# Moving operands of the FFN in six groups of rows, each starting at another remainder of 128 bytes

## The chip, the cores and the metric

The kernel runs on one core of a Trainium2 chip. Times are microseconds (us) of device time for one execution; three timed runs of the kernel before are given with their median, and one further execution was profiled.

## The reference

One decoder block over a sequence of 256 tokens and 2048 channels, all in float32: a conditioning vector gives shift, scale and gate; two token mixers (Mamba-2 SSD and Gated DeltaNet) run in parallel and are merged; then comes the feed-forward part (FFN), with which this case deals:

```python
def swiglu(h, w_gate_up, w_down):
    gate, up = jnp.split(h @ w_gate_up, 2, axis=-1)
    return (jax.nn.silu(gate) * up) @ w_down

h = modulate(rms_norm(x, norm_ffn_w[layer]), shift_f, scale_f)
x = x + gate_f[:, None, :] * swiglu(h, w_gate_up[layer], w_down[layer])
return rms_norm(x, final_norm_w)
```

`h` is 256 x 2048, the hidden width is 5632.

## The kernel before

Activations lie transposed: channels on the 128 partitions, in rows of 256 tokens. A row is 256 float32 values, 1024 bytes on each partition. `h` has 16 rows (KT), the hidden layer 44 (FT).

Each float32 product is made of three matmuls in the type float32r. A weight block `raw` (128 x 1024, eight tiles of 128 x 128) comes in by DMA; ScalarE casts it to `hi` (line 146), VectorE makes the rest `lo = raw - hi` (line 148). The activations are split in the same way, into `h2h` and `h2l` for the first half of the FFN and `fh` and `fl` for the second. For each weight tile and row there are three matmuls, with weights `hi`, `hi`, `lo` as the stationary operand and a row of `h2h`, `h2l`, `h2h` (or `fh`, `fl`, `fh`) as the moving one: lines 216 to 218 in `lin_items`, lines 239 to 241 in `quad_items`. A block is so 24 matmuls. The gate/up half has 176 blocks (`w_gu`; the first twelve by `quad_items`), 4224 matmuls; the down half has 88 (`w_dn`), 2112 matmuls; together 6336.

`ffn_post` (lines 1146 to 1155) works on each of the 44 gate/up pairs when its sum is done: tanh on ScalarE, two products on VectorE, then `A.copy(fh[:, j, :], th)` and `V.tensor_sub(fl[:, j, :], ...)` write row j. Blocks are loaded ahead by `pump` (up to four of them ready), and each engine runs its instructions in the order in which the program gives them.

The tiles of the FFN are made at lines 1176 to 1181, when the pools of the mixers have been closed. A tile `off` of 48 words stands first and shifts all that follow it. By the program's layout the pool `ff` begins at byte 82432 of a partition, a multiple of 512, so that `h2h` starts at 82624, `h2l` at 99008, `fh` at 115392 and `fl` at 160448. Since a row is 1024 bytes, every row of these four tiles starts at remainder 64 of 128. The same remainder holds for the moving operands of the earlier stages: `hh` and `hl` (input projections, lines 216 to 218 as well), `yh` and `yl` (mixer outputs), `mh` and `ml` (merged, for `w_o`). The weight blocks `hi` and `lo` all start at a multiple of 512. In `z_items` (lines 262 to 264) the roles are turned round: there a block of weights is moving, 512 columns of it, at remainder 0.

Lines 1184 to 1191 fill `h2h` and `h2l` row by row: VectorE makes `htmp`, ScalarE writes the row of `h2h`, VectorE that of `h2l`.

Of the kernel before, what the change touches and what calls it, by code (L numbers as in the profile page):

```python
# [10 lines left out]
F32 = mybir.dt.float32  # L11
F32R = mybir.dt.float32r
# [7 lines left out]
P = 128  # L20
D = 2048
S = 256
KT = D // P
# [3 lines left out]
FT = 44  # L27
# [23 lines left out]
NCA = 2  # L51
LZ = 2

OFF = 48

VB_ADA = 0
VN_MIX = 96
# [11 lines left out]
C_NSL = 2  # L69
C_LV = 6  # L70
C_I16 = C_LV * P + 3 * 64


@with_exitstack
def block_kernel(ctx: ExitStack, tc: tile.TileContext, xT, cvec, vec, dskip, consts,
# [44 lines left out]
    def vcol(i):  # L120
        return vs[:, i:i + 1]
# [33 lines left out]
    def pump():  # L155
        while items and len(ready) < LA + 1:
            load_next()
        did = False
        if ready and ready[0][2] <= st_["done"]:
            mm, post, need, sync, hi, lo = ready.popleft()  # L160
            if sync:
                finish_posts()
            mm(hi, lo)
            posts.extend(post)
            st_["mm"] += 1
            did = True
        st_["wait"] -= 1.0
        if st_["gen"] is None and gens and gens[0][1] <= st_["mm"]:
            finish_posts()
            st_["gen"] = gens.popleft()  # L170
            st_["wait"] = 0.0
        if st_["gen"] is not None and (st_["wait"] <= 0.0 or not did):
            try:
                st_["wait"] = max(st_["wait"], -0.99) + next(st_["gen"][0]) * st_["gen"][2]
            except StopIteration:
                st_["gen"] = None
                st_["done"] += 1
        if posts:
            posts.popleft()()
        while len(posts) > PQ:  # L180
            posts.popleft()()
        st_["pumped"] += 1
        if side and st_["side"] and st_["pumped"] % st_["side"] == 0:
            side.popleft()()

    def flush():
        while items or ready or gens or st_["gen"] is not None:
            pump()
        finish_posts()
# [14 lines left out]
    def lin_items(blocks, xh, xl, nk, done, need=0, sync=False, late_need=0):  # L204
        hold = {}
        def mk(bi):
            def mm(hi, lo):
                ah, al = (xh(), xl()) if callable(xh) else (xh, xl)
                if bi == 0:
                    hold["ps"] = plin.tile([P, 2, S], F32, tag="lin", name="ps_lin")  # L210
                ps = hold["ps"]
                for j in range(BLK):
                    t, kt = divmod(bi * BLK + j, nk)
                    s = slice(j * P, (j + 1) * P)
                    h_ = ah[kt // 8][:, kt % 8, :] if isinstance(ah, list) else ah[:, kt, :]
                    T_.matmul(ps[:, t, :], hi[:, s], h_, start=kt == 0, stop=False)  # L216
                    T_.matmul(ps[:, t, :], hi[:, s], al[:, kt, :], start=False, stop=False)  # L217
                    T_.matmul(ps[:, t, :], lo[:, s], h_, start=False, stop=kt == nk - 1)  # L218
            return mm
        for bi, src in enumerate(blocks):  # L220
            last = bi == len(blocks) - 1
            post = [lambda f=f: f(hold["ps"]) for f in done] if last else []
            add_item(src, mk(bi), post, late_need if last and late_need else need, sync and bi == 0)
# [81 lines left out]
    def sq_finish():  # L305
        ps = bank("ps_sq", (P, S))
        for i, k in enumerate("ab"):
            for t in range(2):
                T_.matmul(ps, ones, sqa[k][:, t, :], start=i + t == 0, stop=i + t == 2)
        return ps  # L310

    def rstd_T(pool, ps):
        r = pool.tile([P, S], F32, tag="rstd", name="rstd")
        A.activation(r, ps, AF.Sqrt, scale=1.0 / D, bias=EPS)
        V.reciprocal(r, r)
        return r
# [12 lines left out]
    def ada_fin(j0, j1):  # L329
        V.tensor_tensor(ada[:, j0:j1], ada2[:, j0:j1, 0], ada2[:, j0:j1, 1], ADD)  # L330
        V.tensor_tensor(ada[:, j0:j1], ada[:, j0:j1], vs[:, VB_ADA + j0:VB_ADA + j1], ADD)
# [7 lines left out]
    with tc.tile_pool(name="st", bufs=1) as st:  # L339
# [97 lines left out]
        r = rstd_T(st, ps)  # L437
# [10 lines left out]
        for q in range(1, 4):  # L448
# [9 lines left out]
            if q == 2:  # L458
# [6 lines left out]
                lv = st.tile([P, 3, 64], F32, name="lv")  # L465
                nc.sync.dma_start(lv, consts[:, C_LV * P:C_I16].rearrange("p (a b) -> p a b", b=64))
                V.tensor_copy(lvm, lv)
# [163 lines left out]
    def gdn_mix(hu, unit):  # L631
        if hu == 0:
            pools["gp"] = gs.enter_context(tc.tile_pool(name="gp", bufs=1))
            pools["gsm"] = gs.enter_context(tc.tile_pool(name="gsm", bufs=2))
            pools["i16"] = pools["gp"].tile([64, 256], F32, name="i16")
            nc.sync.dma_start(pools["i16"], consts[0:64, C_I16:C_I16 + 256])
        gp, gsm = pools["gp"], pools["gsm"]
# [485 lines left out]
    def res_post(j, gate, pool):  # L1123
        def f(ps):
            x2 = pools["accs"]
            for t in range(2):
                i = 2 * j + t
                V.scalar_tensor_tensor(x2[:, i, :], ps[:, t, :], gate[:, i:i + 1], x2[:, i, :], MUL, ADD)
            sq = pool.tile([P, 2, S], F32, tag="th" if j else "cacc", name="sq", bufs=1 if j or pool is not gl_ else NCA)
            A.activation(sq, x2[:, 2 * j:2 * j + 2, :], AF.Square)  # L1130
            if j == 0:
                sqa["a"] = sq
            elif j < 7:
                G.tensor_tensor(sqa["a"], sqa["a"], sq, ADD)
            else:
                sqa["b"] = sq
        return [f]
# [36 lines left out]
    phase_a.close()  # L1174

    with tc.tile_pool(name="ff", bufs=1) as ff:
        ff.tile([P, OFF], F32, name="off")
        h2h = ff.tile([P, KT, S], F32R, name="h2h")
        h2l = ff.tile([P, KT, S], F32R, name="h2l")
        fh = ff.tile([P, FT, S], F32R, name="fh")  # L1180
        fl = ff.tile([P, FT, S], F32R, name="fl")
        F_.update(h=h2h, l=h2l, fh=fh, fl=fl, ff=ff)
        tmps = {}
        for t in range(KT + 1):
            if t < KT:
                tmps[t] = ff.tile([P, S], F32, tag="fth", name="htmp", bufs=2)
                V.scalar_tensor_tensor(tmps[t], x2[:, t, :], wsf[:, t:t + 1], rf, MUL, MUL)
                A.activation(h2h[:, t, :], tmps[t], AF.Identity, bias=ada[:, 48 + t:49 + t])
            if t > 0:
                V.scalar_tensor_tensor(h2l[:, t - 1, :], tmps[t - 1], ada[:, 47 + t:48 + t],  # L1190
                                       h2h[:, t - 1, :].bitcast(F32), ADD, SUB)
        while items:
            pump()
        while side:
            side.popleft()()
        gf = ff.tile([P, KT], F32, name="gf")
        for j in range(8):
            lin_items([w_dn[j, b] for b in range(11)], fh, fl, FT, res_post(j, gf, ff))
        ada_fin(80, 96)
        V.tensor_scalar(gf, ada[:, 80:96], 0.5, None, MUL)  # L1200
        while len(items) > 20:
            pump()
        for t in (1, 4, 7):
            A.activation(x2[:, t, :], x2[:, t, :], AF.Identity, scale=vcol(VN_FIN + t))
        A.activation(dum, ones[:, 0:1], AF.Sqrt)
        flush()
        r = rstd_T(ff, sq_finish())
        for t in range(KT):
            if t in (1, 4, 7):
                G.tensor_tensor(x2[:, t, :], x2[:, t, :], r, MUL)  # L1210
            else:
                V.scalar_tensor_tensor(x2[:, t, :], x2[:, t, :], vcol(VN_FIN + t), r, MUL, MUL)
            if t % 2 == 1:
                (nc.sync if t % 4 == 1 else nc.scalar).dma_start(out[:, t - 1:t + 1, :], x2[:, t - 1:t + 1, :])
# [101 lines left out]
```

## Time and profile before

| | us |
|---|---|
| timed runs | 2779.04, 2808.68, 2811.40 |
| their median | 2808.68 |
| the profiled execution | 2783.04 |
| its span (first to last instruction) | 2781.3 |
| TensorE busy in the span | 2673.4 (96%) |
| FFN matmuls, first start to last start | 2037.8 to 2765.9 |

In the profile PE is TensorE's matmul, PEld its weight load, DVE is VectorE, ACT ScalarE, POOL GpSimd. Matmuls are pipelined: the duration of one (276 ns in the FFN) is longer than the distance from its start to the next start. So the pace of the engine is read from starts, and is called the pitch here: the time from one matmul's start to that of the next. The ends of matmuls are modelled.

### The profile page before, as it was taken

What the parts mean: (1) busy time and instruction counts of PE and PEld (TensorE: products, weight loads), DVE (VectorE), ACT (ScalarE), POOL (GpSimd) and SP (SyncE); (2) the same over time, 40 slices, a digit from 0 to 9 for tenths busy, and PEclk for the clock granted to TensorE, in tenths of its full rate; (3) what the DMA queues carried; (4) which work ended last, traced back from release to release, by engine and by line L of the source; (5) the groups of instructions that cost most, each with busy time, mean ns of one, the idle gap of its engine ahead of it and who ended that gap; (6) DMA issues with size and microseconds to landing.
All of it is one profiled execution on the core that took longest, in us unless ns stands there. A gap on an engine that the chain in (4) does not pass through costs nothing.

```text
span 2781.3 us, 51762 instructions
## 1 busy us (share of the span) xinstructions
PE 2673.4 (96%) x20930; PEld 2549.9 (92%) x20930; DVE 1885.3 (68%) x2794; ACT 1372.3 (49%) x2250; POOL 289.3 (10%) x684
## 2 busy tenths in 40 slices
PE   6999999999999999999999999999989999999998
PEld 5998898989899898889898999999989999999997
DVE  6887757667685766767766777777666666655444
ACT  3335454645454454546565565664444444444442
POOL 0000312213021221300000000002100000000000
PEclk8999999999999999999999999999999999999999
DMA  8986646465564646545555555556756666665553
GB/s 324 331 311 213 214 161 223 143 209 170 182 207 152 223 145 207 165 168 172 204 197 186 193 182 183 189 188 240 247 173 229 226 224 232 220 205 196 192 188 137
DMA packets 183283, 566.89 MB, mean 204 GB/s; under 512 B 34754, under 2 KB 43778, under 8 KB 183042
## 3 DMA queue, kind: packets, MB, share of 16 engines
q1 hardware_dynamic: 154306, 552.56, 58.2%
q10 hardware_dynamic: 28736, 11.01, 1.5%
q8 instruction: 164, 2.69, 0.4%
q14 instruction: 77, 0.62, 0.1%
HBM read 552.49 MB, written 11.01 MB: 203 GB/s over the span
## 4 chain that ended last, share of the span: by engine, by line
PE 61%; issue 12%; DVE 11%; POOL 8%; ACT 5%; DMA 3%; SPq 0%; ACTq 0%; DVEq 0%; POOLq 0%
PE ps_lin L216 13%; PE ps_lin L217 13%; PE ps_lin L218 13%; DVE lo L148 4%; PE ps_z L262 3%; PE ps_z L264 2%; PE ps_z L263 2%; POOL tm L726 2%; POOL Gt L728 2%; DVE cacc L290 2%; DMA raw<-in_w_g 1%; ACT hi L146 1%; DVE araw L326 1%; DMA araw<-in_w_ada 1%; PE td L777 1%
## 5 line engine op out<-in xcount | busy, mean ns | idle before, releaser
L148 DVE TENSOR_TENSOR lo<-raw,hi 128x1024 fp32r<-128x1024 f32 x825 | 1010.3, 1235 | 551.1 <-ACT hi L146 544.3
L146 ACT CAST hi<-raw 128x1024 fp32r<-128x1024 f32 x825 | 857.9, 1049 | 479.1 <-PE ps_lin L217 298.9
L216 PE MATMUL ps_lin<-hh,hi 128*128 128x256 f32 x1792 | 507.6, 283 | 1.0 <-DVE accg L574 1.0
L218 PE MATMUL ps_lin<-hh,lo 128*128 128x256 f32 x1792 | 499.6, 279 | 7.4 <-DVE lo L148 7.4
L217 PE MATMUL ps_lin<-hl,hi 128*128 128x256 f32 x1792 | 499.0, 278 | 0.0
L216 PE MATMUL ps_lin<-h2h,hi 128*128 128x256 f32 x1312 | 362.1, 276 | 0.0
L217 PE MATMUL ps_lin<-h2l,hi 128*128 128x256 f32 x1312 | 362.1, 276 | 0.0
L218 PE MATMUL ps_lin<-h2h,lo 128*128 128x256 f32 x1312 | 362.1, 276 | 0.0
L218 PEld LDWEIGHTS ps_lin<-hh,lo 128*128 128x128 f32 x1792 | 338.5, 189 | 8.8 <-DVE lo L148 8.8
L216 PEld LDWEIGHTS ps_lin<-hh,hi 128*128 128x128 f32 x1792 | 338.2, 189 | 5.0 <-issue 3.6
L217 PEld LDWEIGHTS ps_lin<-hl,hi 128*128 128x128 f32 x1792 | 338.8, 189 | 4.0 <-issue 2.6
L216 PE MATMUL ps_lin<-yh,hi 128*128 128x256 f32 x896 | 260.7, 291 | 18.8 <-DVE accg L574 17.0
L217 PE MATMUL ps_lin<-yl,hi 128*128 128x256 f32 x896 | 253.0, 282 | 0.0
L218 PE MATMUL ps_lin<-yh,lo 128*128 128x256 f32 x896 | 252.9, 282 | 0.0
L216 PEld LDWEIGHTS ps_lin<-h2h,hi 128*128 128x128 f32 x1312 | 246.3, 188 | 0.0
L217 PEld LDWEIGHTS ps_lin<-h2l,hi 128*128 128x128 f32 x1312 | 246.3, 188 | 0.0
L218 PEld LDWEIGHTS ps_lin<-h2h,lo 128*128 128x128 f32 x1312 | 246.3, 188 | 0.0
L262 PE MATMUL ps_z<-hi,hh 128*128 128x512 f32 x512 | 208.9, 408 | 2.6 <-DVE zs L273 2.0
L263 PE MATMUL ps_z<-lo,hh 128*128 128x512 f32 x512 | 201.7, 394 | 1.6 <-DVE lo L148 1.6
L264 PE MATMUL ps_z<-hi,hl 128*128 128x512 f32 x512 | 202.5, 396 | 0.0
L218 PE MATMUL ps_lin<-fh,lo 128*128 128x256 f32 x704 | 194.3, 276 | 0.0
L216 PE MATMUL ps_lin<-fh,hi 128*128 128x256 f32 x704 | 194.3, 276 | 0.0
(322 smaller groups left out, 5272.3 us busy)
## 6 DMA issues: line engine op xcount, KB each, us to landing
raw<-in_w_gu SPq DMA_DIRECT2D x176, 512.0 KB, 4.3
raw<-in_w_g SPq DMA_DIRECT2D x143, 512.0 KB, 4.2
raw<-in_w_ada SPq DMA_DIRECT2D x128, 512.0 KB, 4.8
raw<-in_w_s SPq DMA_DIRECT2D x96, 512.0 KB, 4.2
raw<-in_w_dn SPq DMA_DIRECT2D x88, 512.0 KB, 4.2
araw<-in_w_ada SPq DMA_DIRECT2D x64, 512.0 KB, 7.7
raw<-in_w_gz SPq DMA_DIRECT2D x64, 512.0 KB, 4.3
raw<-in_w_gp SPq DMA_DIRECT2D x64, 512.0 KB, 3.7
```

Source lines behind the costliest of these rows:

```text
L146: A.copy(hi, raw)
L148: V.tensor_sub(lo, raw, hi.bitcast(F32))
L216: T_.matmul(ps[:, t, :], hi[:, s], h_, start=kt == 0, stop=False)
L217: T_.matmul(ps[:, t, :], hi[:, s], al[:, kt, :], start=False, stop=False)
L218: T_.matmul(ps[:, t, :], lo[:, s], h_, start=False, stop=kt == nk - 1)
L262: T_.matmul(pss[c], hh[:, kt, cs], hi[:, s], start=kt == 0, stop=False)
L263: T_.matmul(pss[c], hh[:, kt, cs], lo[:, s], start=False, stop=False)
L264: T_.matmul(pss[c], hl[:, kt, cs], hi[:, s], start=False, stop=kt == KT - 1)
L290: V.scalar_tensor_tensor(acc[:, t, j:], x[:, t, :S - j], vcol(cw + 4 * t + 3 - j), acc[:, t, j:], MUL, ADD)
L326: V.scalar_tensor_tensor(raw, raw, 0.5, cact[:, hs], MUL, MUL, accum_out=ada2[:, j, hf:hf + 1])
L726: G.tensor_tensor(t3, F3[:, j + 1:16, j:j + 1].broadcast_to([64, n, j]), G3[:, j:j + 1, 0:j].broadcast_to([64, n, j]), MUL)
L728: G.tensor_tensor(G3[:, j + 1:16, 0:j], G3[:, j + 1:16, 0:j], t3, ADD)
```

## The change

The tile `off` goes. One tile `big` takes the place of `h2h`, `h2l`, `fh` and `fl`. It holds six groups of rows one after the other; a group has a part for the high and a part for the low halves of its rows, and starts at a set remainder: `pos += (rem // 4 - pos) % 128` counts words, so the start is `rem` modulo 512 bytes. A small class `Rows` picks the part in which a row lies, so that all other lines of the program stay as they are.

| rows | start, modulo 512 bytes | matmuls that read them |
|---|---|---|
| hidden rows 0 to 10 | 8 | 528 |
| `h` rows 0 to 7 | 16 | 2112 |
| `h` rows 8 to 15 | 32 | 2112 |
| hidden rows 11 to 21 | 64 | 528 |
| hidden rows 22 to 32 | 96 | 528 |
| hidden rows 33 to 43 | 144 | 528 |

The pool's base stays at 82432. `big` ends at 205456; the two scratch tiles `fth` that follow it move to 205472 and 206496 (before: 205504 and 206528).

```diff
-OFF = 48
+ROWS = [("f", 8), ("h", 16), ("h", 32), ("f", 64), ("f", 96), ("f", 144)]
...
+class Rows:
+    def __init__(self, tiles, n):
+        self.tiles, self.n = tiles, n
+
+    def __getitem__(self, ix):
+        p, r, c = ix
+        return self.tiles[r // self.n][p, r % self.n, c]
...
     with tc.tile_pool(name="ff", bufs=1) as ff:
-        ff.tile([P, OFF], F32, name="off")
-        h2h = ff.tile([P, KT, S], F32R, name="h2h")
-        h2l = ff.tile([P, KT, S], F32R, name="h2l")
-        fh = ff.tile([P, FT, S], F32R, name="fh")
-        fl = ff.tile([P, FT, S], F32R, name="fl")
+        groups = {"h": ([], []), "f": ([], [])}
+        words = sum(2 * S * (KT // 2 if k == "h" else FT // 4) for k, _ in ROWS) + ROWS[-1][1] // 4
+        big = ff.tile([P, words], F32R, name="mov")
+        pos = 0
+        for k, rem in ROWS:
+            pos += (rem // 4 - pos) % 128
+            n = KT // 2 if k == "h" else FT // 4
+            for part in groups[k]:
+                part.append(big[:, pos:pos + n * S].rearrange("p (a b) -> p a b", b=S))
+                pos += n * S
+        assert pos == words
+        h2h, h2l = (Rows(g, KT // 2) for g in groups["h"])
+        fh, fl = (Rows(g, FT // 4) for g in groups["f"])
```

## Rows read from the trace of the kernel before

**Rows 1.** The page: span, busy time, and the chain that ended last by engine.

```profile
span 2781.3 us, 51762 instructions
...
PE 2673.4 (96%) x20930; PEld 2549.9 (92%) x20930; DVE 1885.3 (68%) x2794; ACT 1372.3 (49%) x2250; POOL 289.3 (10%) x684
...
PE 61%; issue 12%; DVE 11%; POOL 8%; ACT 5%; DMA 3%; SPq 0%; ACTq 0%; DVEq 0%; POOLq 0%
```

**Rows 2.** Windows of the FFN, all engines (busy us, number of instructions).

```profile
core 0: us, PE busy (x) PEld busy (x) DVE busy (x) ACT busy (x) POOL busy (x), PEclk, DMA share, GB/s
...
2030.00:2080.00 50.00, 41.67 (x304) 39.46 (x304) 34.71 (x56) 22.55 (x33) 0.00 (x0) 0.86 0.42 146
2080.00:2526.00 446.00, 446.00 (x3938) 446.00 (x3937) 275.57 (x338) 200.86 (x248) 0.00 (x0) 1.00 0.67 222
2526.00:2766.00 240.00, 240.00 (x2120) 240.00 (x2119) 112.81 (x103) 96.42 (x99) 7.77 (x6) 1.00 0.54 179
```

**Rows 3.** Line 217 by operand: duration ns min/median/max, first and last start.

```profile
L217 PE MATMUL ps_lin<-hl,hi x1792: 276/276/415, 306.1 to 1900.4; 128*128 128x256 f32 x200
...
L217 PE MATMUL ps_lin<-h2l,hi x1312: 276/276/276, 2080.7 to 2526.4; 128*128 128x256 f32 x188
...
L217 PE MATMUL ps_lin<-yl,hi x896: 276/281/420, 491.8 to 1872.3; 128*128 128x256 f32 x180
...
L217 PE MATMUL ps_lin<-fl,hi x704: 276/276/276, 2526.8 to 2765.8; 128*128 128x256 f32 x176
```

**Rows 4.** Line 217 again, from 428 to 450.3 us alone.

```profile
L217 PE MATMUL ps_lin<-hl,hi x64: 281/281/281, 427.9 to 450.1; 128*128 128x256 f32 x64
```

**Rows 5.** Line 217 again, from 676 to 692 us alone.

```profile
L217 PE MATMUL ps_lin<-hl,hi x48: 276/276/276, 675.9 to 691.9; 128*128 128x256 f32 x48
```

**Rows 6.** Timeline of PE, two restarts after small matmuls: start us, us, instruction.

```profile
365.63 0.61 PE L804 MATMUL v<-vb,Vm 128*128 128x128 f32 x4
365.99 0.37 PE L216 MATMUL ps_lin<-hh,hi 128*128 128x256 f32 x1
...
366.31 0.28 PE L218 MATMUL ps_lin<-hh,lo 128*128 128x256 f32 x1
...
366.99 0.28 PE L218 MATMUL ps_lin<-hh,lo 128*128 128x256 f32 x1
...
381.82 0.83 PE L868 MATMUL o<-v,QT 128*128 128x128 f32 x6
382.41 0.36 PE L216 MATMUL ps_lin<-hh,hi 128*128 128x256 f32 x1
...
382.73 0.28 PE L218 MATMUL ps_lin<-hh,lo 128*128 128x256 f32 x1
...
383.78 0.28 PE L218 MATMUL ps_lin<-hh,lo 128*128 128x256 f32 x1
```

**Rows 7.** Timeline of PE, runs of other matmuls (merged; duration from first start to last end).

```profile
63.20 2.10 PE L388 MATMUL ps_q<-x,whole 128*128 128x256 f32 x9
...
299.63 1.04 PE L733 MATMUL qt<-cst,E 128*128 128x128 f32 x8
```

**Rows 8.** Durations of these two kinds: ns min/median/max.

```profile
L388 PE MATMUL ps_q<-x,whole x240: 377/379/381, 63.2 to 191.8; 128*128 128x256 f32 x120
...
L733 PE MATMUL qt<-cst,E x64: 270/273/273, 299.6 to 1156.1; 128*128 128x128 f32 x64
```

**Rows 9.** Tile h2h, and fh: who writes and reads them, and when.

```profile
L239 PE MATMUL ps_lin<-h2h,hi x96: 276/276/579, 2037.8 to 2080.2; 128*128 128x256 f32 x96
...
L1188 ACT ACTIVATE h2h<-htmp,ada x16: 494/508/511, 2037.3 to 2050.7; 128x256 fp32r<-128x256 f32 x16
L1190 DVE SCALAR_TENSOR_TENSOR h2l<-htmp,ada,h2h x16: 477/479/485, 2037.8 to 2051.2; 128x256 fp32r<-128x256 f32 x16
...
L1153 ACT CAST fh<-fth x44: 405/407/408, 2076.7 to 2528.2; 128x256 fp32r<-128x256 f32 x44
L1154 DVE TENSOR_TENSOR fl<-fth,fh x44: 424/426/427, 2077.1 to 2528.6; 128x256 fp32r<-128x256 f32 x44
```

**Rows 10.** Groups from 2085 to 2526 us: the rest of `ffn_post`; busy, mean ns | idle before.

```profile
L1151 DVE SCALAR_TENSOR_TENSOR fth<-fth,ps_lin 128x256 f32<-128x256 f32 x40 | 16.8, 421 | 35.8 <-ACT fth L1150 35.8
L1152 DVE TENSOR_TENSOR fth<-fth,ps_lin 128x256 f32<-128x256 f32 x40 | 16.8, 420 | 1.4
...
L1150 ACT ACTIVATE fth<-ps_lin 128x256 f32<-128x256 f32 x40 | 15.4, 384 | 69.5 <-PE ps_lin L218 69.5
```

**Rows 11.** Waits from 2085 to 2766 us: in total, times, longest.

```profile
ACT hi L146 <- PE ps_lin L217: 244.1, 147, 1.7
DVE lo L148 <- ACT hi L146: 226.8, 188, 2.4
```

## The prediction

> **What bounds the kernel now.** I read the page first. The reader is to see that TensorE is busy for 96% of the span and that the chain which ended last is mostly PE [rows 1]. Next come the windows of the FFN: from 2080 to 2766 us PE is busy in every microsecond at the full granted clock, 1.00, while VectorE and ScalarE work 275.57 and 200.86 of the 446 us of the gate/up half, and the DMA engines 0.67 of it [rows 2]. The waits agree: ScalarE waits for PE to free a weight buffer, 244.1 us in total, and no wait of PE is among the long ones [rows 11]. So in this stage a nanosecond more or less on each matmul goes straight into the time, and nothing else does. It touches only the FFN, whose matmuls are 6336.
>
> Then the pitch, from first and last starts. Line 217 is every third matmul. In the gate/up half (2526.4 - 2080.7) / 1311 / 3 = 113.3 ns; in the down half (2765.8 - 2526.8) / 703 / 3 = 113.3 ns [rows 3]. All durations there are 276 ns, the median and the maximum.
>
> The earlier stages show that this pitch is not the only one. From 427.9 to 450.1 us the same instruction, on `hl` at the same remainder 64 and with the same shapes, took (450.1 - 427.9) / 63 / 3 = 117.5 ns, and every duration is 281 [rows 4]. From 675.9 to 691.9 us it is (691.9 - 675.9) / 47 / 3 = 113.5 ns, which is the 113.3 within the rounding of the starts, and 276 [rows 5]. The timeline shows how one is chosen: after a few small matmuls the stream at 366.31 goes on at (366.99 - 366.31) / 6 = 113 ns, the one at 382.73 at (383.78 - 382.73) / 9 = 117 ns [rows 6]. Tile, remainder and weights' place are of the same kind in both. So there are two paces, a restart picks one, and it then lasts. Over all of line 217, `hl` has a median of 276 and `yl` one of 281 [rows 3]: about half of those matmuls went at the long pitch, while all of the FFN of this execution went at the short one.
>
> The step between the paces is 117.5 - 113.3 = 4.2 ns, in the FFN 6336 x 4.14 (before rounding) = 26 us. The profiled execution took 2783.0 us (its span 2781.3, and 1.7 around it). With the whole FFN at the long pitch it would have taken 2783 + 26 = 2809. Two of the three timed runs, 2808.68 and 2811.40, lie there and the third, 2779.04, lies by the profiled one. This fits, and is not shown: no trace of those runs stands here.
>
> **The change, part by part.** What it adds and removes in instructions: nothing. Each matmul, cast and load has the same shape and place in its queue. The tile `off` has no instruction. `fth` moves by 32 bytes; the engines that use it are half idle in that stage [rows 2], and a slower access of theirs is hidden behind PE until the 0.38 to 0.43 us operations of `ffn_post` have grown several times, since five of them fall on each 10.9 us of matmuls (the 96 of a pair at 113.3 ns) [rows 9, 10].
>
> One tile in place of four could add waits, if dependences were kept by tile. They are kept by rows: matmuls on `h2h` start at 2037.8 us, while later rows of the same tile are still written until 2050.7 [rows 9]. I take nothing for it. If that cover were gone, see the third rival.
>
> What is left is the start of the rows. Of the 6336 matmuls 528 keep remainder 64; 5808 get another (all 4224 of gate/up, and 1584 of down). No row shows a float32r row of 256 columns at any remainder but 64, so the price per matmul has to be bounded.
>
> Below: the shortest pitch with weights of this size. Eight transposes of 128 columns take 1.04 us in all, the last one 273 ns: (1040 - 273) / 7 = 110 ns [rows 7, 8]. That would be a gain of 3.7 ns on each, at most 6336 x 3.7 = 23 us.
>
> Above: the only matmuls of 256 columns that read the same number of bytes at a longer pitch are those in plain float32: (2100 - 379) / 8 = 215 ns [rows 7, 8]. That would be 102 ns more on 5808 matmuls, 591 us. It is another type of product, and so far from the case; I keep it as the end of the unknown alone.
>
> Nearest: the two paces of the very same instruction, 0 to 4.2 ns more [rows 3, 4]. I take a value between these two. A change of remainder comes with every block in gate/up (rows 0 to 7, then 8 to 15) and with every eleven rows in down, and I expect that it disturbs the stream as a restart does, so that the pace is drawn again and again. In the stages where it is often redrawn about half the matmuls had the long one [rows 3]. So 6336 x 4.14 x 0.5 = 13 us: 2783 + 13 = 2796.
>
> [...] The row gives 113.3 ns [rows 3]. [...]
>
> **The rivals.**
>
> The start has no influence. Then the FFN has one pace from its start to its end, as in the profiled execution, and the time is 2783 or 2809, by whichever it falls into. For it: two paces appear at one and the same remainder, so the remainder is not what makes them [rows 4, 5]. Against it: nothing, but it leaves open what a change of start within the stream does.
>
> A start off 64 costs time itself. [...] At the price of one step, 4.2 ns, it is 5808 x 4.2 = 24 us: 2807; at two steps 2831. It ends slower by more than 2% from (2865 - 2783) / 5808 = 14 ns on each, over three steps. For it: nothing shows those starts, and the bound above is high [rows 7]. [...]
>
> Waits by tile. If writing a row of `fh` into `big` held up the matmuls that read `h` out of `big`, PE would stand for the chain of `ffn_post` after each of 44 pairs: 384 + 421 + 420 + 407 + 426 ns = 2.06 us [rows 9, 10], 91 us in all, 2874, slower by over 2%. It decides from 1.9 us a pair. Against it: matmuls and writes of one tile run side by side now [rows 9].
>
> A gain. If some of the new starts bring the pitch to the 110 ns of the transposes, the time is 2783 - 23 = 2760. For it: PE takes a weight load of this size and a matmul in that time [rows 7, 8]. Against it: 256 columns never did in this trace. [...]
>
> **How the numbers follow.** Paces mixed, 2785 to 2807: 0.46. One pace throughout: the short one, 2778 to 2785, 0.17; the long one, 2807 to 2813, 0.16. A cost of the start itself: 2813 to 2835, 0.07; 2835 to 2865, 0.04; above 2865, 0.04. Waits by tile: 0.03. A gain: 0.03. The prediction is 2796, with the first case's own range 2783 to 2809. The range 2772 to 2835 leaves out the gain, the waits and the dearer starts, 0.14. Two per cent, about what a measurement of this kernel can tell from no change, is 56 us around 2808.68: from 2752 to 2865. The gain doesn't reach that; I leave it 0.01. Slower: 0.04 + 0.03 = 0.07. Same: 0.92.
>
> **What would show it.** Pitches by group of rows tell nearly all. If the steps are right, `h` rows 0 to 7 and 8 to 15 and the four groups of hidden rows show only the two paces, 113.3 and 117.5 ns, with durations of 276 and 281, and both occur within the FFN. One pace in all groups speaks for the first rival; a pace fixed to a group, and beyond 118 ns, for the second; idle PE after each pair for the third; a group under 113 ns for the gain. PE must still be busy for all of 2080 to 2766 us, and the time up to 2037 us must be as before within a few us; if the mixers' stages differ by more than that, the comparison is disturbed by what the change doesn't touch. The forecast is wrong if any group runs above 122 ns, twice the step.

## The result and the profile after

| | kernel before | changed kernel |
|---|---|---|
| median, 20 runs each | 2782.51 | 2807.26 |
| lowest and highest | 2777.16, 2811.40 | 2801.71, 2811.34 |
| span of the profiled execution | 2781.3 | 2805.9 |
| FFN, first start to last start | 2037.8 to 2765.9 | 2037.7 to 2790.5 |

The ratio is 1.0056, with a 95% interval from 1.0032 to 1.008: slower by half a per cent. The medians lie further apart, 24.8 us or 0.9%, because the runs of the kernel before fall into two clusters, 13 of the 20 between 2777 and 2787 and 7 between 2808 and 2812. The changed kernel has one, at 2807. The three runs shown ahead of the prediction were one of the lower cluster and two of the upper.

The windows of the FFN in the changed kernel (columns as in [rows 2]):

```profile
core 0: us, PE busy (x) PEld busy (x) DVE busy (x) ACT busy (x) POOL busy (x), PEclk, DMA share, GB/s
2030.00:2080.00 50.00, 42.54 (x308) 40.41 (x307) 35.14 (x57) 22.57 (x34) 0.00 (x0) 0.90 0.44 149
2080.00:2526.00 446.00, 446.00 (x3825) 446.00 (x3825) 267.78 (x325) 196.58 (x242) 0.00 (x0) 1.00 0.65 216
2526.00:2790.00 264.00, 264.00 (x2222) 264.00 (x2222) 120.22 (x113) 101.30 (x106) 7.77 (x6) 1.00 0.51 172
```

PE is still busy all the time at full granted clock, 1.00, but in the same 446 us it does 3825 matmuls and not 3938. The wait of ScalarE for PE grew with it, from 244.1 us [rows 11] to this (from 2085 to 2790 us, a window 24 us longer):

```profile
ACT hi L155 <- PE ps_lin L226: 264.0, 149, 1.8
```

So nothing became idle: each matmul takes longer. Line 226 is the 217 of before, on all of the new tile (ns min/median/max, first and last start):

```profile
L226 PE MATMUL ps_lin<-mov,hi x2016: 277/280/286, 2080.2 to 2790.4; 128*128 128x256 f32 x184
```

(2790.4 - 2080.2) / 2015 / 3 = 117.5 ns, against 113.3 [rows 3]. Over these 6048 matmuls the step is 25 us, and the spans differ by 24.6. None of these has the 276 ns that all of them had before.

The timeline gives the pitch of each group. These are the first matmuls of three blocks in gate/up, and of the four groups of a pass in the down half (the last line begins the next pass):

```profile
2304.05 0.28 PE L225 MATMUL ps_lin<-mov,hi 128*128 128x256 f32 x1
...
2306.85 0.28 PE L225 MATMUL ps_lin<-mov,hi 128*128 128x256 f32 x1
...
2309.65 0.28 PE L225 MATMUL ps_lin<-mov,hi 128*128 128x256 f32 x1
...
2602.05 0.28 PE L225 MATMUL ps_lin<-mov,hi 128*128 128x256 f32 x1
...
2606.00 0.28 PE L225 MATMUL ps_lin<-mov,hi 128*128 128x256 f32 x1
...
2609.89 0.28 PE L225 MATMUL ps_lin<-mov,hi 128*128 128x256 f32 x1
...
2613.84 0.28 PE L225 MATMUL ps_lin<-mov,hi 128*128 128x256 f32 x1
...
2617.76 0.28 PE L225 MATMUL ps_lin<-mov,hi 128*128 128x256 f32 x1
```

A block is 24 matmuls: 2.80 / 24 = 116.7 ns at start 16, and the same at 32. A group of hidden rows is 33: 119.7 at 8, 117.9 at 64, 119.7 at 96, 118.8 at 144. Summed, with 3936 matmuls at 3.4 ns over 113.3 and 528 each at 6.4, 4.6, 6.4 and 5.5, this is 25.5 us. The rows at 64, which by the prediction's count kept their start, are long too.

### The profile page after: what moved, and what is told of

The parts are those of the page before. It is cut to its first block, busy times and chain, and to the rows that moved or that the text cites. A ratio compares the mean times of both kernels' runs of the same rounds, so it can differ in the third digit from the quotient of the medians.

```text
span 2805.9 us, 51762 instructions
## 1 busy us (share of the span) xinstructions
PE 2702.3 (96%) x20930; PEld 2578.2 (92%) x20930; DVE 1886.8 (67%) x2794; ACT 1373.1 (49%) x2250; POOL 290.7 (10%) x684
## 4 chain that ended last, share of the span: by engine, by line
PE 61%; issue 12%; DVE 11%; POOL 8%; ACT 5%; DMA 2%; SPq 0%; ACTq 0%; DVEq 0%; POOLq 0%
PE ps_lin L225 14%; PE ps_lin L227 13%; PE ps_lin L226 13%; DVE lo L157 4%; PE ps_z L271 3%; PE ps_z L273 3%; PE ps_z L272 3%; POOL tm L735 2%; POOL Gt L737 2%; DVE araw L335 2%; DVE cacc L299 2%; ACT hi L155 1%; PE td L786 1%; PE tw L778 1%; DMA raw<-in_w_g 1%
## 5 line engine op out<-in xcount | busy, mean ns | idle before, releaser
L225 PE MATMUL ps_lin<-mov,hi 128*128 128x256 f32 x2016 | 563.8, 280 | 0.0
L226 PE MATMUL ps_lin<-mov,hi 128*128 128x256 f32 x2016 | 563.4, 279 | 0.0
L227 PE MATMUL ps_lin<-mov,lo 128*128 128x256 f32 x2016 | 563.1, 279 | 0.0
L227 PEld LDWEIGHTS ps_lin<-mov,lo 128*128 128x128 f32 x2016 | 379.7, 188 | 0.0
L226 PEld LDWEIGHTS ps_lin<-mov,hi 128*128 128x128 f32 x2016 | 379.3, 188 | 0.0
L225 PEld LDWEIGHTS ps_lin<-mov,hi 128*128 128x128 f32 x2016 | 379.1, 188 | 0.0
L225 PEld LDWEIGHTS ps_lin<-yh,hi 128*128 128x128 f32 x896 | 173.2, 193 | 23.7 <-issue 20.3
L299 DVE SCALAR_TENSOR_TENSOR cacc<-ps_lin,vs,cacc 128x255 f32<-128x255 f32 (+2 forms) x288 | 138.3, 480 | 64.8 <-ACT cacc L296 57.3
```

The source lines that it names most:

```text
L299: V.scalar_tensor_tensor(acc[:, t, j:], x[:, t, :S - j], vcol(cw + 4 * t + 3 - j), acc[:, t, j:], MUL, ADD)
```

## The experiments

In all kernels but two only the list of starts differs from the changed kernel. Pitches are worked out as above, from first and last start of line 226 over 2015 steps of three matmuls. The kernel before ran beside each group of them.

**One start for all rows: 64, 0, 16, 32.**

```diff
-ROWS = [("f", 8), ("h", 16), ("h", 32), ("f", 64), ("f", 96), ("f", 144)]
+ROWS = [("f", 64), ("h", 64), ("h", 64), ("f", 64), ("f", 64), ("f", 64)]
```

and likewise with 0, 16 and 32.

> The changed kernel with all six groups at 64. Three theories stand. Own pitch: each start has its own pitch (in the changed kernel 8: 119.8 ns, 16 and 32: 116.7, 96: 119.7), and only 64 has the short one beside the long one. Disturbance: a change of start within the stream keeps it at the long pitch, and any start used alone has both. Structure: the one tile in place of four is the cause, or the new distances between high and low rows. Own pitch and disturbance expect what the kernel before shows: runs near 2780 or near 2809, a single pitch of 113.3 or 117.5 ns in the whole FFN. Structure expects 2807 in all runs and no run below 2800.

> All six groups at 0. No run has shown a row of 256 columns at 0. Own pitch: some one value in all rows of the FFN, from 113.3 to 120 ns, the same in all runs; at 113.3 always it would be 2780 in all runs and so beat both kernels, at 117.5 2809. Disturbance: 2780 or 2809 by the run, as at 64. Structure: 2807.

> All six groups at 16, no change of start within the FFN. Own pitch: 116.7 ns in every row of gate/up and of down, 2780 + 6336 x 3.3 = 2801 us in all runs. Disturbance: 113.3 or 117.5 ns, runs near 2780 or 2809. Structure: 2807.

> All six groups at 32. Own pitch: 116.7 ns throughout, 2801 us in all runs. Disturbance: 113.3 or 117.5 ns, runs near 2780 or 2809. Structure: 2807.

Measured, line 226 at 64, at 0, at 16 and at 32:

```profile
L226 PE MATMUL ps_lin<-mov,hi x2016: 279/279/279, 2086.5 to 2798.4; 128*128 128x256 f32 x184
```

```profile
L226 PE MATMUL ps_lin<-mov,hi x2016: 283/283/283, 2086.0 to 2811.4; 128*128 128x256 f32 x184
```

```profile
L226 PE MATMUL ps_lin<-mov,hi x2016: 277/278/280, 2079.8 to 2785.1; 128*128 128x256 f32 x184
```

```profile
L226 PE MATMUL ps_lin<-mov,hi x2016: 277/278/281, 2080.6 to 2785.8; 128*128 128x256 f32 x184
```

| start | pitch in the profile, ns | runs | median, us | ratio, 95% interval |
|---|---|---|---|---|
| 64 | 117.8 | 1 at 2777, 11 from 2806 to 2816 | 2808.34 | 1.0051, 1.0012 to 1.009 |
| 0 | 120.0 | 12 from 2819 to 2829 | 2822.56 | 1.0119, 1.0085 to 1.0153 |
| 16 | 116.7 | 4 from 2780 to 2782, 6 from 2802 to 2814 | 2801.99 | 1.0016, 0.997 to 1.0063 |
| 32 | 116.7 | 10 from 2800 to 2807 | 2804.69 | 1.0052, 1.0013 to 1.009 |

Disturbance falls: at 0 and at 32 nothing changes within the FFN, and no run is short. A start has paces of its own: in these runs one (0, 32) or two (16, 64, by the clusters). The pitch sets the time: 0 is 6048 x 6.7 = 40 us above 2781, and 2822 was measured. One thing didn't fit: at 64, the remainder of the kernel before modulo 128, nearly all runs are long, while its own are mostly short. Modulo 512 it stands at 192.

**All rows at 192; only rows 0 to 10 at 8; all at 8; weights moved.**

```diff
+ROWS = [("f", 192), ("h", 192), ("h", 192), ("f", 192), ("f", 192), ("f", 192)]
...
+ROWS = [("f", 8), ("h", 192), ("h", 192), ("f", 192), ("f", 192), ("f", 192)]
...
+ROWS = [("f", 8), ("h", 8), ("h", 8), ("f", 8), ("f", 8), ("f", 8)]
```

The fourth kernel has `ROWS` all at 0 and one more line ahead of the first tile, which moves all tiles by 64 bytes:

```diff
+    const.tile([P, 16], F32, name="pad")
     cact = const.tile([P, D], F32, name="cact")
```

> All six groups at 192, which is where the four tiles of the kernel before start modulo 512 (64 modulo 128). All six at 64 ran long (117.8 ns) in most runs, the kernel before short (113.3 ns) in most. Two theories. Modulo 512: 192 and 64 differ, and the share of short runs goes with the start; then this kernel does as the kernel before, about three runs in four near 2780 and the rest near 2809. Structure: what lowers the share of short runs is the one tile with its other distances between high and low rows; then this kernel does as the one at 64: nearly all runs near 2808.

> Hidden rows 0 to 10 at 8, all others at 192; only 528 of the 6336 matmuls have another start. Own pitch: 120 ns in these 528 and 113.3 elsewhere, 2780 + 528 x 6.5 = 2783 us in the runs that begin short. Disturbance: gate/up at the short pitch in such a run, but the first pass over the rows at 8 throws the stream over and it stays long in the rest of the down half, as the rows at 64 of the changed kernel do (117.8 ns): 2780 + 528 x 6.5 + 1584 x 4.4 = 2790. Where gate/up is long from the start both give some 2810.

> A tile of 64 bytes ahead of everything: the weight blocks hi and lo move from remainder 0 to 64 of 512, the operands of the mixers from 192 to 256, and the FFN's rows, all in one group class at the pool's base, stand at 64. So rows and weights have the same remainder, as in the kernel with all rows at 0, but both 64 bytes on. If what counts is where the moving rows start: 113.3 or 117.8 ns as in the kernel with all rows at 64, times near 2780 or 2808. If what counts is how the moving row stands to the weights: 120.0 ns in all rows, 2822 us in all runs, and the mixers as before.

> All six groups at 8. Own pitch: near 119.8 ns in all rows, as the rows at 8 have in the changed kernel, 2780 + 6336 x 6.5 = 2821 us in all runs. If those rows were long there only because the stream had been disturbed ahead of them: some runs at 113.3 ns, near 2780.

Measured, line 226 with all rows at 192, with the line for `ml`, the moving operand of the stage ahead:

```profile
L226 PE MATMUL ps_lin<-mov,hi x2016: 276/276/276, 2084.3 to 2769.4; 128*128 128x256 f32 x184
...
L226 PE MATMUL ps_lin<-ml,hi x160: 281/281/281, 1981.2 to 2037.4; 128*128 128x256 f32 x160
```

113.3 ns, eleven runs of twelve from 2778 to 2791 and one at 2809, ratio 1.0007 (0.9983 to 1.0031). This is the kernel before again. The one tile and its distances cost nothing, so the theory called structure falls, and the start counts modulo more than 128: modulo 128 it is the same as 64, where all rows had 117.8 ns. In this execution `ml` was long, (2037.4 - 1981.2) / 159 / 3 = 117.8 ns, and the FFN behind it short, both at 192: the pace was drawn anew at the start of the FFN.

With rows 0 to 10 at 8 the timeline of a pass is:

```profile
2587.02 0.28 PE L225 MATMUL ps_lin<-mov,hi 128*128 128x256 f32 x1
...
2590.91 0.28 PE L225 MATMUL ps_lin<-mov,hi 128*128 128x256 f32 x1
...
2594.67 0.28 PE L225 MATMUL ps_lin<-mov,hi 128*128 128x256 f32 x1
...
2598.41 0.28 PE L225 MATMUL ps_lin<-mov,hi 128*128 128x256 f32 x1
```

3.89 / 33 = 117.9 ns at 8, 113.9 in the first group behind it, 113.3 in the next. The stream is not thrown over for good: the rows at 192 draw it back within that group. All ten runs lie from 2782 to 2792, ratio 0.9994 (0.9967 to 1.002).

With all rows at 8, and with weights and rows both at 64, line 226 (227 in the second) is:

```profile
L226 PE MATMUL ps_lin<-mov,hi x2016: 277/277/278, 2082.5 to 2792.9; 128*128 128x256 f32 x184
```

```profile
L227 PE MATMUL ps_lin<-mov,hi x2016: 283/283/283, 2085.6 to 2811.0; 128*128 128x256 f32 x184
```

At 8 it is 117.5 ns, six runs from 2805 to 2813, ratio 1.0087 (1.0057 to 1.0117). The changed kernel had 119.7 in its rows at 8 and the one above 117.9, so the value is not quite the start's own; the neighbours weigh in. The changed kernel shows it within one execution: in the first pass of the down half, entered from the rows of `h`, its rows at 8 take 3.89 / 33 = 117.9 ns, and in the 15 passes entered from rows at 144 they take 119.9 on average.

```profile
2539.25 0.28 PE L225 MATMUL ps_lin<-mov,hi 128*128 128x256 f32 x1
...
2543.14 0.28 PE L225 MATMUL ps_lin<-mov,hi 128*128 128x256 f32 x1
```

With the weights moved too it is 120.0 ns in all matmuls, four runs from 2821 to 2830, ratio 1.014 (1.0093 to 1.0186): just as with rows and weights both at 0, though the rows stand at 64, where they had 117.8 with the weights at 0. What counts is the start of the moving row against that of the weights. The stages ahead of the FFN in the same execution say so too. By the program's layout their moving operands stand at 256 there, against weights at 64, so 192 apart as before. With weights at 0, rows at 256 had 119.6 ns (below). Here both paces of the kernel before appear again (line 227 on `hl` has a median of 276 ns and on `yl` one of 280, against 276 and 281), and `ml` runs at (2035.9 - 1981.8) / 159 / 3 = 113.4 ns:

```profile
L227 PE MATMUL ps_lin<-ml,hi x160: 276/276/276, 1981.8 to 2035.9; 128*128 128x256 f32 x160
```

So where the weights lie changes the pitch of the stream, by 2.2 ns at least between this kernel, at 120.0, and the one with all rows at 64, at 117.8 (all other tiles moved by the same 64 bytes); how it does so, no run shows.

**Rows 0 to 10 at 64, and twelve more starts in two kernels.**

```diff
+ROWS = [("f", 64), ("h", 192), ("h", 192), ("f", 192), ("f", 192), ("f", 192)]
...
+ROWS = [("f", 128), ("h", 160), ("h", 224), ("f", 256), ("f", 320), ("f", 384)]
...
+ROWS = [("f", 48), ("h", 80), ("h", 112), ("f", 208), ("f", 240), ("f", 416)]
```

> Hidden rows 0 to 10 at 64, all others at 192. With all rows at 64 most runs were long, at 192 most were short. If a start has its own pitch and draws the stream into it: 117.8 ns in the rows at 64 and 113.3 in the rows at 192 behind them, 2780 + 528 x 4.4 = 2782. If at 64 both paces hold on and the entry decides: the rows at 64 go at 113.3 ns too when the gate/up half was short.

> Six other starts at once, as the changed kernel has it: hidden rows at 128, 256, 320 and 384, rows of h at 160 and 224. Own pitch: each group has its own mean from 113.3 to 120 ns that can be read by group, and the time is their sum over 6336 matmuls. If only the remainder of 128 counted, 128, 256 and 384 would be at 120 as the rows at 0, 320 would be at 117.8 as those at 64, 160 at 116.7 as those at 32. A group at 113.3 ns is a candidate for a kernel that stays short.

> Six more: hidden rows at 48, 208, 240 and 416, rows of h at 80 and 112. Own pitch: a mean of its own in each group, 113.3 to 120 ns, and the time their sum. Next to 192, 208 is expected short if the pitch changes slowly with the start.

Measured, a pass with the rows at 64:

```profile
2587.56 0.28 PE L225 MATMUL ps_lin<-mov,hi 128*128 128x256 f32 x1
...
2591.44 0.28 PE L225 MATMUL ps_lin<-mov,hi 128*128 128x256 f32 x1
...
2595.19 0.28 PE L225 MATMUL ps_lin<-mov,hi 128*128 128x256 f32 x1
...
2598.93 0.28 PE L225 MATMUL ps_lin<-mov,hi 128*128 128x256 f32 x1
```

3.88 / 33 = 117.6 ns at 64, entered from rows at 113.3, then 113.6 and 113.3 again. So the start draws the stream: to the long pace at 64, to the short one at 192. Eight of ten runs lie from 2781 to 2787, two at 2805 and 2815; ratio 0.9999 (0.9952 to 1.0045).

In the first kernel of six starts no group comes near 113.3. From all starts in its trace the means are 118.6 at 128, 118.0 at 160, 118.2 at 224, 119.6 at 256, 117.9 at 320 and 118.7 at 384; eight runs from 2806 to 2815, ratio 1.0061 (1.0014 to 1.0108). That 256 lies by 0 (119.6 and 120.0) and 320 by 64 (117.9 and 117.8; and 416, in the next kernel, by 160: 118.0 both) speaks for a count modulo 256; 192 and 64 (113.3 and 117.8) exclude 128. In the second kernel the rows of `h` differ (80, then 112):

```profile
2303.50 0.28 PE L225 MATMUL ps_lin<-mov,hi 128*128 128x256 f32 x1
...
2306.38 0.28 PE L225 MATMUL ps_lin<-mov,hi 128*128 128x256 f32 x1
...
2309.10 0.28 PE L225 MATMUL ps_lin<-mov,hi 128*128 128x256 f32 x1
```

2.88 / 24 = 120.0 ns at 80 and 2.72 / 24 = 113.3 at 112, turn about through the whole gate/up half. The hidden rows at 48, 208, 240 and 416 have means from 117.1 to 118.4. So 208 at 118.0 is not short, as it was expected to be next to 192, at least in this company. Eight runs from 2803 to 2807, ratio 1.0062 (1.0023 to 1.01).

**All rows at 112, then the mixers too.**

```diff
+ROWS = [("f", 112), ("h", 112), ("h", 112), ("f", 112), ("f", 112), ("f", 112)]
```

The second kernel adds pads and slices that bring `hh`, `hl`, `yh` and `yl` to 112 modulo 256:

```diff
-    hh = ap_.tile([P, KT, S], F32R, name="hh")
-    hl = ap_.tile([P, KT, S], F32R, name="hl")
+    ap_.tile([P, 40], F32, name="pad")
+    hb = ap_.tile([P, 2 * KT * S + 8], F32R, name="hb")
+    hh, hl = (hb[:, 4 + i * KT * S:4 + (i + 1) * KT * S].rearrange("p (a b) -> p a b", b=S) for i in range(2))
```

> All six groups at 112, the one start that stayed at 113.3 ns in the midst of a group at 120. Own pitch: 113.3 ns in every row and every run, no run above 2795, median 2780 against some 2782 of the kernel before, whose runs lie in two clusters. If 112 too has a long pace besides, some runs lie near 2805 to 2810 as before.

> As the kernel with all rows at 112, and the moving operands of the mixers' stages, hh, hl, yh and yl, moved from 192 to 112 modulo 256 as well (pads ahead of them; mh, ml and the weights stay). If the start against the weights sets the pitch wherever such matmuls stand: no more long stretches of lines 216 to 218 ahead of 1900 us; some 3800 of the 9000 matmuls there are long in the kernel before, 3800 x 4.3 ns = 16 us less, near 2764. If the long stretches there come from the small matmuls of the mixers between them and not from the start: the same share stays long and the time is 2780.

Measured, line 226 of the first, then of the second (where `hb` holds `hh` and `hl`, `y` both `yh` and `yl`):

```profile
L226 PE MATMUL ps_lin<-mov,hi x2016: 275/275/275, 2073.3 to 2758.4; 128*128 128x256 f32 x184
```

```profile
L226 PE MATMUL ps_lin<-hb,hi x1792: 275/275/415, 303.9 to 1900.4; 128*128 128x256 f32 x200
L226 PE MATMUL ps_lin<-y,hi x896: 275/275/420, 488.9 to 1872.2; 128*128 128x256 f32 x180
```

All rows at 112: 113.3 ns, twelve runs from 2776 to 2790 and none in the upper cluster (nor any of the twelve of the second kernel), median 2781.42; the kernel before beside it had three of 23 there. Over all five groups of runs 29 of its 128 lie above 2800. The ratio, 0.9982 (0.9953 to 1.0011), is no measured gain.

In the mixers the median of `y` is 275 where `yl` had 281 [rows 3], and stretches of 40 or more matmuls in a row at 116 to 121 ns, some 35 of them ahead of 1900 us in the kernel before, are gone. So the start sets the pace there too. But the time isn't lower: median 2782.78, ratio 0.9992 (0.9966 to 1.0017), and the FFN begins at 2037.7 as before. Lines 271 to 273 have `hh` and `hl` as stationary operands against weights that move. A stretch of them in this kernel, then in the kernel before:

```profile
250.28 0.39 PE L271 MATMUL ps_z<-hi,hb 128*128 128x512 f32 x1
...
251.68 0.39 PE L271 MATMUL ps_z<-hi,hb 128*128 128x512 f32 x1
```

```profile
249.75 0.39 PE L262 MATMUL ps_z<-hi,hh 128*128 128x512 f32 x1
...
251.12 0.39 PE L262 MATMUL ps_z<-hi,hh 128*128 128x512 f32 x1
```

1.40 / 6 = 233 ns against 1.37 / 6 = 228. Over all that follow one another closely (distances under 300 ns) the means are 233.7 and 229.5; there are 1536 of these matmuls, so 6.4 us more in all. The saving itself was also smaller than the expected 16 us. On the 9235 matmuls that read `hh`, `hl`, `yh` or `yl` ahead of 1900 us the mean distance of starts, those over 140 ns left out, went from 115.3 to 114.3 ns, about 9 us. For one, after an interruption some matmuls still go at the long pitch. Here ten went at (572.88 - 571.70) / 10 = 118 ns, on rows at 112, where the median duration is the short 275 ns:

```profile
571.70 0.28 PE L225 MATMUL ps_lin<-hb,hi 128*128 128x256 f32 x1
...
572.88 0.28 PE L226 MATMUL ps_lin<-hb,hi 128*128 128x256 f32 x1
```

The two nearly cancel.

## Why the prediction was wrong

**The frame held.** PE is the bound of the FFN in both kernels, PE has no wait of its own there (busy in 446.00 of the 446 us from 2080 to 2526 in both), and what the change does it does by the pitch, 117.5 ns for 113.3. Nothing moved ahead of 2037 us: the FFN begins at 2037.7.

**The base was wrong.** The prediction added its 13 us to the profiled execution, 2783, and compared the 2796 with a median of 2808.68: a loss by the one, a small gain by the other. It said itself that two of the three runs lay where the whole FFN would be at the long pitch, and its profile at the other. More runs put the kernel before at 2782.5. From there 2796 is a loss, as the sum had it, and the true step is 24.8 us. That the upper cluster is the long pitch in the FFN is still not seen in a trace of the kernel before, but a kernel that has both clusters (all at 64) showed 117.8 ns through the whole FFN in an execution of the upper one.

**The step that failed is the price of a start**, "I take a value between these two". It held that a changed start disturbs the stream, so that the short and the long pace are redrawn and each takes half: 13 us. The runs show that a start against the weights fixes which paces there are and draws the stream to them within the group (117.6 ns at 64, then 113.6 and 113.3 at 192), and that none of the six chosen starts holds the short one in that company, 64 included: 25.5 us for 13. The half was high as well: of the 2686 matmuls of line 217 on `hl` and `yl` ahead of 1900 us 1034 had the 281 ns of the long pace, some four in ten. And the count of 528 that keep their start goes by 128 bytes; by the 256 that the runs speak for, 192 became 64 there and no row kept its start.

The second rival had the right kind of cause, a cost of the start itself, and with 5808 x 4.2 = 24 us the 2807 that was measured; it got 0.15 in three parts, none of them as low as 2807. That the number fits so well is in part luck: it charged nothing for the rows at 64, which cost 4.6 ns each, and 4.2 for the rows of `h`, which cost 3.4. What the prediction said for the first rival, that two paces at one remainder make the remainder not the cause, was the error: one start can have two paces and another start one.

The second rival's condition, a start off 64, is refuted: 64 itself ran at 117.8 ns and long in eleven runs of twelve, 0 and 256 cost as much as any (120.0 and 119.6), and 112 is short (113.3).

**First rival** (the start has no influence): refuted by the rows at 0, 120.0 ns in all matmuls and no run below 2818.9. **Waits by tile**: refuted by all rows at 192, where the same one tile runs at 113.3 ns over all 2016 matmuls of line 226, with no stop after a pair. **A gain**: no start went under 113.3 ns, the floor of all that was tried. The 110 ns of the transposes [rows 7, 8] was not reached by any.

**What it named as a sign against itself** didn't come: no group above 122 ns, the highest mean of the changed kernel 119.9. But both paces within the FFN, the sign for it, didn't come either: on lines 225 to 227 no matmul of the changed kernel's FFN had 276 ns.

## What to carry to other kernels

When TensorE is the bound and weights are loaded for every matmul, read the pitch from starts, stage by stage, before anything else: from the shortest start to the longest it moved here by 6.7 ns on each of 6048 matmuls, 40 us of 2781. Where the moving operand starts against the stationary one is worth a sweep, several starts in one kernel by groups and then the best one alone, since neighbours weigh in (rows at 8 took 117.9 ns behind rows of `h` and 119.9 behind rows at 144). And when runs fall into two clusters, count them before taking three of them as the base.

## What was not expected of the hardware

The pitch of a 256-column float32r matmul with its weight load went from 113.3 to 120.0 ns with the start of the moving row, counted from that of the weights: 120.0 at 0 and at 80 bytes, 116.7 to 117.8 at 8, 16, 32 and 64, 113.3 at 112 and in most runs at 192. Moving rows and weights together by 64 bytes left the 120.0 as it was. At 16, 64 and 192 the runs fall into two clusters, 23, 32 (by a single short run) and 29 us apart, and what picks one at the start of the FFN stays open. So does why 112 is short (113.3 ns) while 80, 128 and 96 beside it are not (120.0, 118.6 and 119.7).
